# Two 64-byte gaps that shift the weights' split tiles off the 128-byte lines of SBUF

## The chip, the cores and the metric

The kernel runs on one core of a Trainium2 chip. The metric is the device time of one execution in microseconds (us), of which several are taken. Engines are named as in the profile: PE is TensorE's matmul, PEld its weight load, DVE is VectorE, ACT is ScalarE, POOL is GpSimd, SP issues the DMAs.

## What is computed

A decoder trunk of two layers on 256 positions with 1024 features, in float32. Layer 0 mixes tokens by dilated attention (16 heads, three groups of windows), layer 1 by an mLSTM block. After each mixer come an MLP with a squared ReLU and a gated input embedding.

```python
for i in range(2):
    if i == 0:
        x = x + dilated_attention(rms_norm(x, a_norm), a_w_qkv, ..., a_w_o)
    else:
        x = x + mlstm_mixer(rms_norm(x, b_norm), b_w_up, ..., b_w_down)
    x = x + jnp.square(jax.nn.relu(rms_norm(x, mlp_norm[i]) @ mlp_w1[i])) @ mlp_w2[i]
    gate = jax.nn.sigmoid(rms_norm(x, ple_norm[i]) @ ple_w_gate[i])
    x = x + gate * (p[i] @ ple_w_proj[i])
```

All the weights together are 138 units of 128 partitions by 2048 float32 (1 MB each). They are read from HBM once and used once, so the kernel is a long stream of weights past a small set of activations.

## The kernel before

**The stream of weights.** `dma(u)` (L161) brings unit u into one of three buffers `raw`. `split(u, c)` (L166) cuts a unit's 512-column piece into two float32r parts: ACT copies it to `hi` (L176), and DVE subtracts to get `lo` (L177). Twelve buffers each of `hi` and `lo` hold three units. One piece is a slot, and `open_slot` / `close_slot` (L209, L218) count slots: a split runs 7 slots ahead of its use during the attention projections and 11 afterwards. Work that isn't part of the stream (attention, gates, norms) is hung on slots with `at(slot, f)`.

**The products.** An activation h is kept as two parts as well (`hh` and `hl`, `hidh` and `hidl`, and so on), and each product is made of three matmuls: hi times hh, hi times hl, lo times hh. `stream` (L318) does this for most of the kernel. The weights' 128x128 piece is the stationary operand (512 bytes in a partition, loaded anew for every matmul), and the activation is the moving one (256 columns, 1024 bytes):

```python
mm(acc[:, q], wh, h, ...)   # L331
mm(acc[:, q], wh, l, ...)   # L332
mm(acc[:, q], wl, h, ...)   # L333
```

In the attention projections `qkv_block` (L483; matmuls on L499 to L501) it is the other way round: the activation is stationary, and the weights move, 512 columns at a time.

**The order.** A list of units written by hand sets it: `qkv` (36 units, slots with attention work between), `proj0`, `woA` and `woB` (the attention's output projection, moving operand `oT`), `w1_0` (moving `hh`), `w2_0` (moving `hid`), `gate0` (moving `hG`), `xm`, `z0` to `z3` (moving `hh`), `wd0` (moving `hB`), `proj1`, `wd1` (`hh`), `w1_1` (`hB`), `w2_1` (`hid`), `gate1` (`hh`). PE works through it in program order.

**Where the tiles lie.** Pools are laid out one after another from the bottom of SBUF: `base` (parameters, `hh`, `hl` and others), then `raw`, `hi`, `lo`, then the pool `sq`, and above it the pools of the stages in turn. A tile's start in a partition follows from the sizes before it. In the program as built, these are the starts of the rows counted modulo 128 bytes, for the operands of the matmuls:

| rows | used in | before | after the change |
|---|---|---|---|
| `hi`, `lo` (weights) | everywhere | 0 | 64 |
| `raw` | input of the split | 0 | 0 |
| `hh`, `hl` | qkv, w1_0, xm, z, wd1, gate1 | 0 | 0 |
| `hidh`, `hidl` | w2_0, w2_1 | 0 | 0 |
| `hBh`, `hBl` | wd0, w1_1 | 0 | 0 |
| `hWh`, `hWl` | four units of qkv | 0 | 0 |
| `oTh`, `oTl` | woA, woB | 64 | 64 |
| `hGh`, `hGl` | gate0 | 96 | 96 |
| `pT` (two parts) | proj0 / proj1 | 96 / 32 | 96 / 32 |

Every tile of these has rows that are whole multiples of 512 bytes, and so do the slices of them, so that a matmul's operand begins where its tile begins, modulo 128. Counted modulo 256 bytes, the distance from a row of weights to a row of activations (activation minus weights) was 0 for `hh`, `hid`, `hB` and `hW` and 192 for `oT`. After the change it is 192 for `hh`, 64 for `hid`, `hB` and `hW`, and 0 for `oT`.

Of the kernel before, what the change touches and what calls it, by code (L numbers as in the profile page):

```python
# [10 lines left out]
F32 = mybir.dt.float32  # L11
# [7 lines left out]
D, S, P = 1024, 256, 128  # L19
# [9 lines left out]
UC = 2048  # L29
HU = 512  # L30
# [102 lines left out]
def build(tc, a):  # L133
    nc = tc.nc
    ctx = ExitStack()
    with ctx:
        _build(ctx, tc, nc, a)


def _build(ctx, tc, nc, a):  # L140
    def pool(n, b=1, c=ctx, **k):
        if "space" not in k:
            k["reuse_waits"] = "tile"
        return c.enter_context(tc.tile_pool(name=n, bufs=b, **k))

    base = pool("base")
    rawp, hip, lop = pool("raw", 3), pool("hi", 3 * UC // HU), pool("lo", 3 * UC // HU)
    psa = pool("psa", 3, space=PSUM)
    pst = pool("pst", 2, space=PSUM)
    pss = pool("pss", 2, space=PSUM)  # L150
# [8 lines left out]
    raw, hi, lo = {}, {}, {}  # L159
# [188 lines left out]
    atp = pool("attn", c=actx)  # L348
# [170 lines left out]
    def scores(qt, i):  # L519

        pair, b = divmod(i, 2)
        tb = slice(b * P, (b + 1) * P)
        (qh, ql), (kh, kl) = QT[qt, 0], KTt[qt, 0]
        two = [(slice(r * HD, r * HD + HD), pss.tile([P, 512], F32, name="sc")[:, 0:SC]) for r in range(2)]
        for q, k, first, last in ((qh, kh, True, False), (qh, kl, False, False), (ql, kh, False, True)):
            for r, ps in two:
                mm(ps[:, 0:256], q[r, pair, tb], k[r, pair], start=first, stop=last)  # L527
        for n in range(2):
            for e in range(2):
                t4 = slice(b * P + 64 * e, b * P + 64 * e + 64)  # L530
                g = 1 + (n + e) % 2
                for r, ps in two:
                    mm(ps[64 * e:64 * e + 64, 256 + 64 * n:320 + 64 * n], QT[qt, g][0][r, pair, t4], KTt[qt, g][0][r, pair, t4],  # L533
                       start=True, stop=True)
        for r in range(2):
            j, ps = 2 * pair + r, two[r][1]
            sc = atp.tile([P, SC], F32, name="scs", bufs=2)
            m = atp.tile([P, 4], F32, name="m", bufs=8)
            slope = float(np.float32(2.0 ** (-8.0 * (4 * qt + j + 1) / H)))
            dve.tensor_tensor_reduce(sc, ps, nd[:, b], slope, -3e38, ALU.add, ALU.max, m[:, 0:1])  # L540
            dve.tensor_scalar(m[:, 1:2], m[:, 0:1], -1.0, None, op0=ALU.mult)
            act(sc, sc, AF.Exp, bias=m[:, 1:2], accum_out=m[:, 2:3])
            INST[qt, 2 * j + b] = (sc, m)
# [38 lines left out]
    def attend(qt, t0, step):  # L582
        for i in range(4):
            at(t0 + int((2 * i + 1) * step) + LV, values, qt, i)
        for i in range(4):
            for r in range(2):
                at(t0 + int((2 * i + r) * step) + LT, turn, qt, 4 * (i // 2) + 2 * r + i % 2)
        for i in range(4):
            at(t0 + int(2 * i * step), scores, qt, i)
        at(t0 + int(7 * step) + LV + 1, heads_done, qt)  # L590
# [484 lines left out]
```

## Time and profile before

| | |
|---|---|
| median of 3 runs | 923.03 us (921.54 to 923.29) |
| the profiled execution | 921.63 us, of which 919.9 us from the first to the last instruction |
| granted clock of TensorE, mean over the span | 0.997 of 2.4 GHz |
| PE busy / DVE busy / ACT busy | 98% / 72% / 62% of the span |
| read from HBM | 148 MB, 162 GB/s over the span |

A matmul's record in the profile is longer than the time until the next one starts, since matmuls are pipelined. What a matmul costs a stream that doesn't wait is therefore read as the step from one start to the next, not as the duration of one record.

### The profile page before, as it was taken

What the parts mean: (1) busy time and instruction counts of PE and PEld (TensorE: products, weight loads), DVE (VectorE), ACT (ScalarE), POOL (GpSimd) and SP (SyncE); (2) the same over time, 40 slices, a digit from 0 to 9 for tenths busy, and PEclk for the clock granted to TensorE, in tenths of its full rate; (3) what the DMA queues carried; (4) which work ended last, traced back from release to release, by engine and by line L of the source; (5) the groups of instructions that cost most, each with busy time, mean ns of one, the idle gap of its engine ahead of it and who ended that gap; (6) DMA issues with size and microseconds to landing.
All of it is one profiled execution on the core that took longest, in us unless ns stands there. A gap on an engine that the chain in (4) does not pass through costs nothing.

```text
span 919.9 us, 17609 instructions
## 1 busy us (share of the span) xinstructions
PE 904.3 (98%) x6924; PEld 844.3 (92%) x6924; DVE 659.7 (72%) x1409; ACT 569.5 (62%) x1055; POOL 41.5 (5%) x77
## 2 busy tenths in 40 slices
PE   8799999999999999999999999999999999999997
PEld 6687787877889999999999899999999999999997
DVE  6966877857866866665667987568898666656664
ACT  7567576575585766654446686668866666644442
POOL 0400000000000000000000542000000000000000
PEclk9999999999999999999999999999999999999999
DMA  8744443544443555555555433343265555555521
GB/s 302 281 142 160 156 144 133 178 136 145 154 161 105 178 185 183 184 183 184 183 184 183 157 129 104 127 138 98 87 220 204 184 183 184 184 183 182 184 94 46
DMA packets 23122, 150.23 MB, mean 163 GB/s; under 512 B 2560, under 2 KB 3200, under 8 KB 5632
## 3 DMA queue, kind: packets, MB, share of 16 engines
q1 hardware_dynamic: 23040, 149.12, 47.1%
q8 instruction: 54, 0.88, 0.4%
q14 instruction: 28, 0.23, 0.1%
HBM read 148.06 MB, written 1.05 MB: 162 GB/s over the span
## 4 chain that ended last, share of the span: by engine, by line
PE 92%; DVE 6%; ACT 1%; issue 1%; DMA 0%; SPq 0%; ACTq 0%
PE acc L331 21%; PE acc L332 21%; PE acc L333 21%; PE acc L499 6%; PE acc L501 6%; PE acc L500 6%; DVE lo L177 2%; PE tp L451 1%; PE tp L552 1%; PE sm L570 1%; PE sc L527 1%; PE tp L741 1%; PE tp L751 1%; PE sc L882 1%; PE sc L759 1%; PE sc L533 1%
## 5 line engine op out<-in xcount | busy, mean ns | idle before, releaser
L177 DVE TENSOR_TENSOR lo<-raw,hi 128x512 fp32r<-128x512 f32 x552 | 375.6, 691 | 176.7 <-ACT hi L176 175.3
L176 ACT ACTIVATE hi<-raw 128x512 fp32r<-128x512 f32 x552 | 339.2, 628 | 227.1 <-PE acc L332 204.4
L331 PE MATMUL acc<-hh,hi 128*128 128x256 f32 x640 | 184.0, 288 | 0.3 <-ACT hh L298 0.2
L332 PE MATMUL acc<-hl,hi 128*128 128x256 f32 x640 | 181.5, 284 | 0.1
L333 PE MATMUL acc<-hh,lo 128*128 128x256 f32 x640 | 181.4, 283 | 0.0
L331 PE MATMUL acc<-hidh,hi 128*128 128x256 f32 x512 | 144.9, 283 | 0.0
L332 PE MATMUL acc<-hidl,hi 128*128 128x256 f32 x512 | 144.9, 283 | 0.0
L333 PE MATMUL acc<-hidh,lo 128*128 128x256 f32 x512 | 144.9, 283 | 0.0
L331 PEld LDWEIGHTS acc<-hh,hi 128*128 128x128 f32 x640 | 122.4, 191 | 1.6 <-issue 0.7
L332 PEld LDWEIGHTS acc<-hl,hi 128*128 128x128 f32 x640 | 122.5, 191 | 0.7 <-DVE hl L299 0.5
L333 PEld LDWEIGHTS acc<-hh,lo 128*128 128x128 f32 x640 | 122.4, 191 | 0.0
L499 PE MATMUL acc<-hi,hh 128*128 128x512 f32 x264 | 109.6, 416 | 0.0
L500 PE MATMUL acc<-lo,hh 128*128 128x512 f32 x264 | 104.1, 394 | 0.8 <-DVE lo L177 0.8
L501 PE MATMUL acc<-hi,hl 128*128 128x512 f32 x264 | 104.2, 395 | 0.0
L331 PEld LDWEIGHTS acc<-hidh,hi 128*128 128x128 f32 x512 | 98.3, 192 | 0.0
L332 PEld LDWEIGHTS acc<-hidl,hi 128*128 128x128 f32 x512 | 98.3, 192 | 0.0
L333 PEld LDWEIGHTS acc<-hidh,lo 128*128 128x128 f32 x512 | 98.3, 192 | 0.0
L331 PE MATMUL acc<-hBh,hi 128*128 128x256 f32 x320 | 90.9, 284 | 0.0
L332 PE MATMUL acc<-hBl,hi 128*128 128x256 f32 x320 | 90.7, 283 | 0.0
L333 PE MATMUL acc<-hBh,lo 128*128 128x256 f32 x320 | 90.6, 283 | 0.0
L331 PEld LDWEIGHTS acc<-hBh,hi 128*128 128x128 f32 x320 | 61.4, 192 | 0.3 <-issue 0.3
L332 PEld LDWEIGHTS acc<-hBl,hi 128*128 128x128 f32 x320 | 61.4, 192 | 0.0
(258 smaller groups left out, 1384.3 us busy)
## 6 DMA issues: line engine op xcount, KB each, us to landing
raw<-w SPq DMA_DIRECT2D x136, 1024.0 KB, 4.9
raw<-w SPq DMA_DIRECT2D x8, 256.0 KB, 6.8
x<-x SPq DMA_DIRECT2D x4, 256.0 KB, 5.4
pj<-rep SPq DMA_DIRECT2D x1, 896.0 KB, 6.9
out<-u SPq DMA_DIRECT2D x3, 256.0 KB, 2.4
pT<-p SPq DMA_DIRECT2D x2, 256.0 KB, 4.0
nd<-nd SPq DMA_DIRECT2D x1, 384.0 KB, 6.2
out<-u SPq DMA_DIRECT2D x2, 128.0 KB, 1.9
```

The costliest lines, as they stand in the source:

```text
L176: act(hi[n][:, d], raw[u][:, s], AF.Copy)
L177: dve.tensor_tensor(lo[n][:, d], raw[u][:, s], hi[n][:, d], op=ALU.subtract)
L331: mm(acc[:, q], wh, h, start=first, stop=False, skip_group_check=n > 1)
L332: mm(acc[:, q], wh, l, start=False, stop=False, skip_group_check=n > 1)
L333: mm(acc[:, q], wl, h, start=False, stop=last, skip_group_check=n > 1)
L451: nc.tensor.transpose(ps[:, pair, b * P:(b + 1) * P], n[:, b, ty * 256 + pair * P:ty * 256 + (pair + 1) * P], ident)
L499: mm(accs[b], hh, wh, start=(k == 0), stop=False)
L500: mm(accs[b], hh, wl, start=False, stop=False)
L501: mm(accs[b], hl, wh, start=False, stop=(k == 7))
L527: mm(ps[:, 0:256], q[r, pair, tb], k[r, pair], start=first, stop=last)
L533: mm(ps[64 * e:64 * e + 64, 256 + 64 * n:320 + 64 * n], QT[qt, g][0][r, pair, t4], KTt[qt, g][0][r, pair, t4], start=True, stop=True)
L552: nc.tensor.transpose(psf[:, k * P:(k + 1) * P], pe[:, k * P:(k + 1) * P], ident)
```

## The change

A tile of 64 bytes in a partition (16 float32) that nobody uses is put ahead of the pools of `hi` and `lo`, and a second one behind them. All rows of `hi` and `lo` then begin 64 bytes higher, and all tiles above them 128 bytes higher. To make room for the 128 bytes, the small tile `m` of the attention's softmax (row maximum, its negative, sum, reciprocal), of which there were eight with one head each, becomes four with two heads each. No instruction is added, removed or moved on any engine, and each waits on the same semaphores as before.

```diff
     base = pool("base")
-    rawp, hip, lop = pool("raw", 3), pool("hi", 3 * UC // HU), pool("lo", 3 * UC // HU)
+    rawp = pool("raw", 3)
+
+    pool("gap0").tile([P, 16], F32, name="gap0")
+    hip, lop = pool("hi", 3 * UC // HU), pool("lo", 3 * UC // HU)
+    pool("gap1").tile([P, 16], F32, name="gap1")
     psa = pool("psa", 3, space=PSUM)
...
+        ms = atp.tile([P, 2, 4], F32, name="m", bufs=4)
         for r in range(2):
-            j, ps = 2 * pair + r, two[r][1]
+            j, ps, m = 2 * pair + r, two[r][1], ms[:, r]
             sc = atp.tile([P, SC], F32, name="scs", bufs=2)
-            m = atp.tile([P, 4], F32, name="m", bufs=8)
             slope = float(np.float32(2.0 ** (-8.0 * (4 * qt + j + 1) / H)))
```

## Rows read from the trace of the kernel before

**Rows 1.** The page's busy times of the engines.
```profile
PE 904.3 (98%) x6924; PEld 844.3 (92%) x6924; DVE 659.7 (72%) x1409; ACT 569.5 (62%) x1055; POOL 41.5 (5%) x77
```

**Rows 2.** The page's chain that ended last, shares of the span by engine.
```profile
PE 92%; DVE 6%; ACT 1%; issue 1%; DMA 0%; SPq 0%; ACTq 0%
```

**Rows 3.** Windows: start:end, length, busy of PE, PEld, DVE, ACT, POOL; clock, DMA, GB/s.
```profile
7.50:70.00 62.50, 56.43 (x253) 45.34 (x252) 49.46 (x116) 40.02 (x78) 12.66 (x21) 0.97 0.68 247
70.00:196.00 126.00, 126.00 (x826) 100.39 (x825) 94.50 (x250) 83.08 (x172) 0.00 (x0) 1.00 0.43 149
...
302.00:395.00 93.00, 93.00 (x775) 93.00 (x776) 67.82 (x111) 58.54 (x102) 0.00 (x0) 1.00 0.53 182
395.00:487.00 92.00, 92.00 (x769) 92.00 (x768) 55.09 (x90) 46.00 (x76) 0.00 (x0) 1.00 0.53 183
...
648.00:706.00 58.00, 58.00 (x477) 57.26 (x476) 52.42 (x116) 43.23 (x77) 0.00 (x0) 1.00 0.49 169
```

**Rows 4.** The chain in order of time: start, us, engine and work.
```profile
57.81 0.69 DVE nqk L443
...
503.75 1.44 DVE xn L697 x3
```

**Rows 5.** Line 331 in 395.5 to 487 (w2_0): duration min/median/max, first and last start.
```profile
L331 PEld LDWEIGHTS acc<-hidh,hi x255: 192/192/192, 395.4 to 486.8; 128*128 128x128 f32 x128
L331 PE MATMUL acc<-hidh,hi x255: 283/283/283, 395.5 to 486.9; 128*128 128x256 f32 x128
```

**Rows 6.** Line 331 in 294 to 301 (the end of the output projection, oT).
```profile
L331 PE MATMUL acc<-oTh,hi x21: 276/276/276, 293.9 to 300.7; 128*128 128x256 f32 x21
L331 PEld LDWEIGHTS acc<-oTh,hi x21: 187/188/188, 294.1 to 300.9; 128*128 128x128 f32 x21
```

**Rows 7.** Timeline of PE, a run of oT between attention work: start, us, work.
```profile
286.14 0.28 PE L332 MATMUL acc<-oTl,hi 128*128 128x256 f32 x1
...
287.32 0.28 PE L333 MATMUL acc<-oTh,lo 128*128 128x256 f32 x1
```

**Rows 8.** Line 331 over the whole output projection (270 to 301.7).
```profile
L331 PE MATMUL acc<-oTh,hi x64: 276/276/384, 270.3 to 301.4; 128*128 128x256 f32 x64
```

**Rows 9.** Line 331 in 489 to 499 (gate0, hG).
```profile
L331 PE MATMUL acc<-hGh,hi x27: 278/282/364, 488.7 to 499.0; 128*128 128x256 f32 x27
```

**Rows 10.** Timeline of PE in qkv, 16 steps on end.
```profile
243.48 0.39 PE L500 MATMUL acc<-lo,hh 128*128 128x512 f32 x1
...
247.15 0.39 PE L501 MATMUL acc<-hi,hl 128*128 128x512 f32 x1
```

**Rows 11.** The page's costliest groups: line engine op, count, busy, mean ns, idle before.
```profile
L177 DVE TENSOR_TENSOR lo<-raw,hi 128x512 fp32r<-128x512 f32 x552 | 375.6, 691 | 176.7 <-ACT hi L176 175.3
...
L331 PE MATMUL acc<-hh,hi 128*128 128x256 f32 x640 | 184.0, 288 | 0.3 <-ACT hh L298 0.2
...
L331 PE MATMUL acc<-hidh,hi 128*128 128x256 f32 x512 | 144.9, 283 | 0.0
...
L500 PE MATMUL acc<-lo,hh 128*128 128x512 f32 x264 | 104.1, 394 | 0.8 <-DVE lo L177 0.8
...
L331 PE MATMUL acc<-hBh,hi 128*128 128x256 f32 x320 | 90.9, 284 | 0.0
```

**Rows 12.** DVE's groups with shapes kept apart, two with 512 columns.
```profile
L264 DVE TENSOR_TENSOR sqa<-sqa,sqt 128x512 f32<-128x512 f32 x18 | 12.5, 695 | 0.3
...
L929 DVE TENSOR_TENSOR zt<-acc,rb 128x512 f32<-128x512 f32 x8 | 5.5, 682 | 0.5 <-PE acc L333 0.5
```

**Rows 13.** Timeline of PE at its longest wait: start, us, work, idle before.
```profile
44.89 0.45 PE L451 MATMUL tp<-ident,nqk 128*128 128x128 f32 x1 [5.02 <-DVE nqk L443]
```

## The prediction

> **What bounds the kernel now.** I read the page's busy times first: PE is busy for 98% of the span, with DVE at 72% and ACT at 62% [rows 1]. A busy PE alone proves little, so the chain that ended last comes next: 92% of it is PE, and DVE has 6% [rows 2]. The chain in order of time shows where that 6% lies: its DVE pieces stand before 58 us, and again for a short stretch around 500 to 516 us in `gate0` [rows 4]. Up to 45 us PE even stands still for 5.0 us behind DVE's `nqk` [rows 13], so nothing that PE wins before that point survives. From about 57 us on, PE is the bound. The windows by stage say how much room the others have there: in `w2_0` DVE works 55.1 of 92 us, in `w1_0` 67.8 of 93, in the attention projections 94.5 of 126. The tightest is the stretch from 648 to 706 with 52.4 of 58, that is 90% [rows 3]. So the time is a count of matmuls times the step from one to the next, and the question is what the change does to the step.
>
> **The step, and what the place of the rows has to do with it.** In `w2_0`, line 331 starts 255 times between 395.5 and 486.9 us; 254 rounds of three matmuls in 91.4 us are 762 steps of 120.0 ns. All its records have the same duration, 283 ns, and the weight loads 192 [rows 5]. At the end of the output projection the same line, with the same shapes and the same splits on DVE and ACT, starts 21 times from 293.9 to 300.7 us: 60 steps in 6.8 us, 113.3 ns each, with records of 276 and loads of 188 ns [rows 6]. The engines' clock was granted at 1.00 in both, which is 2.4 GHz. In the table of tiles the one thing that differs is that `oT` begins 64 bytes off the weights' lines, where `hid` begins on them. In qkv 512 columns take 16 steps in 3.67 us, 229.4 ns each [rows 10]. Against the 256 columns of `w2_0`, 256 columns more cost about 109 ns, so that a step of 120.0 holds some 11 to 13 ns over its columns, and `oT` loses about half of that.
>
> I take this as the mechanism: a weight load reads its row while the matmul before it reads its activation's row, and the two get in each other's way less when the rows stand 64 bytes apart modulo 128. The change puts `hh`, `hid` and `hB` where `oT` stood, and `oT` where they stood.
>
> The Trainium skill speaks against this. Its page "TensorE: Matmul & The Clock Gate", section "Part 2: What happens when you issue a matmul", says that loading the next tile's weights takes no read bandwidth of SBUF from the running matmul; its section "Back-to-back issue gap" would put an isolated matmul of 256 columns at 256/2.4 + 2.5 = 109 ns. By that rule both rows above would show 109, and the change would be worth nothing. The trace shows 120.0 and 113.3.
>
> **`oT` has a second rhythm.** A run between pieces of attention work goes from 286.14 to 287.32 us in 10 steps, which are 118 ns each [rows 7]. Which one a run falls into is set by how it starts, after a transpose or a small product, and it stays in it until the next interruption. Over the 192 matmuls of that stage [rows 8] about a quarter of the steps that follow each other closely are at 118, and the rest at 113.3. I take 0.75 x 113.3 + 0.25 x 118 = 114.5 ns for a stream 64 bytes apart. All fast would be 113.3, all slow 118. In the long undisturbed streams (`w1` and `w2`) one of them may hold for a whole stage, and no row tells which.
>
> **The change part by part.**
>
> *Streams whose activations start on the lines.* `hh` has 640 rounds, `hid` 512, `hB` 320 [rows 11]; with three matmuls each, 4416. Their mean records are 283 to 288 ns, as in `w2_0`, so they all run at 120.0. The gain is 4416 x (120.0 - 114.5) = 24.3 us; all fast 29.6, all slow 8.8.
>
> *The attention projections.* Line 500 has 264 matmuls on `hh` [rows 11], with 16 on `hW` and 8 into another buffer, so 288 on each of three lines, 864 in all; 700 of them start after 57 us. Here the weights move, and the activation is loaded, as far apart as `oT` was. No row has 512 columns at that distance: the gain lies between nothing and the 6.7 ns of the smaller matmul, as both have one weight load per matmul. I take the same 5.5, nearer to the row: 3.9 us (0 to 4.7). The 164 before that gain nothing, since DVE sets the end there [rows 13].
>
> *`oT`.* Its 64 rounds [rows 8] now stand on the weights' lines: 192 x (120.0 - 114.5) = 1.1 us lost (0.4 to 1.3).
>
> *`hG` and `pT`.* `hG` moves from 96 to 32 bytes apart. It now takes 26 rounds from 488.7 to 499.0 us [rows 9], 78 steps with two short waits, and its records lie between 276 and 283 like both others. 32 bytes could cost anything between 113.3 and 120.0: 0 to 1.3 us for 192 matmuls, and I take 0.4. The 96 matmuls of `pT` swap 32 for 96 in one layer and 96 for 32 in the other, and I put them at nothing (0.3 us either way).
>
> *The splits.* ACT and DVE now write, and DVE reads, rows at 64. DVE's subtract takes 691 ns with both operands at 0 [rows 11]; with one operand from PSUM a pass of 512 columns takes 682, with both from SBUF 695 [rows 12]. The place of the rows can hardly be worth more than that difference of 13 ns. PE's steps cover it: a slot of 12 matmuls falls from 1440 to 1374 ns, and `w2_0` would still have DVE at 55.1 of 88 us. Without that cover, 60 splits in the first 57 us would cost or give 0.8 us. I put it at nothing.
>
> *DVE's stretch.* From 500 to 516 us the chain goes over DVE [rows 4], and some 130 of the steps counted above gain nothing there: 0.5 us less.
>
> *The tile `m`* keeps its four pairs of buffers, and no wait is added. The DMA has to bring 1 MB in 5.5 instead of 5.76 us in `w1_0`, 191 GB/s for 182; it moved 247 GB/s between 7.5 and 70 us [rows 3]. Between 648 and 706 us PE would need 55.3 us and DVE 52.4, so PE still leads, barely.
>
> Sum: -24.3 - 3.9 + 1.1 - 0.4 + 0.5 = -27.0 us. The profiled execution's 921.63 us become 894.6. It stands 1.4 us under the median of the runs, so that 895 to 896 is the forecast; I say 895.
>
> **The rivals.**
>
> *The slow rhythm everywhere.* If the long streams settle at 118, the gain is 8.8 us there and 700 x 2 = 1.4 in qkv, less 0.4 for `oT`, and the time is about 913. For it: runs of ten steps held it to their end [rows 7]. Against it: the long run at the end of the stage was at 113.3 throughout [rows 6]. Chance 0.10.
>
> *Half of it.* If the distance counts modulo 256, then `oT` at 192 shows what `hh` will do, but nothing shows `hid` and `hB` at 64. If 64 is no better than 0, the 1920 matmuls of `hh` gain 10.6 us and qkv 3.9, `oT` loses 1.1, and the time is about 909. Against it: an exchange of the two rows should not matter. Chance 0.14.
>
> *No change.* If `oT` was fast for another reason, its own values or its place between other work, steps stay at 120 and the time at 923. Against it: DVE, ACT and DMA did the same work beside `oT` [rows 6] as elsewhere. It is also what the Trainium skill's page "SBUF — State Buffer", section "Specifications (TRN2)", suggests, where SBUF's lines are 16 bytes, of which 64 is a multiple; the 120.0 and 113.3 disagree with it as far as the tiles' places are their cause. Chance 0.05.
>
> *Slower.* A loaded row of 512 bytes covers four lines of 128 when it begins on one, and five when it doesn't. If the 13.3 ns over the columns are a price per line of the load, 3.3 each, the step becomes 123.3 and 4416 x 3.3 = 14.6 us are added, with 2.3 for the moving rows of qkv: 940. It decides as soon as `w1_0` shows steps over 120. Every load of `hi` or `lo` in the trace begins on a line, so no row of theirs excludes it; but `oT` moves 9 lines for 8 and was the faster one. Chance 0.06.
>
> **How the numbers follow.** The forecast has 0.65, and its own range goes from all fast in every stage (888) to half of the runs slow (about 901). Half of it and the slow rhythm reach to 909 and 913. The range from 888 to 912 takes in the first three cases but for their edges, some 0.85. A measurement of this kernel tells about 0.2%, 1.8 us, from no change. Forecast, slow rhythm and half make faster 0.89, the third rival same 0.05, the last slower 0.06.
>
> **What would show it.** In the profile after, `w2_0` should take about 87 us between the same units instead of 92, with steps of 113.3 and records of 276 and 188 ns, or 118 in whole stages. qkv should step at about 223 ns, `oT` at 120 with records of 283. PE stays at 97 or 98%, and DVE's split at 691. The prediction is wrong if `w1_0` and `w2_0` differ (then the distance counts modulo more than 128), if `oT` stays at 113.3 (then its place was not the cause), or if steps shrink and waits on `lo` or `hi` take what they gave.

## The result, and the profile after

The changed kernel takes 911.24 us (median of 4 runs, 909.07 to 913.14) against 922.43 us: a ratio of 0.9878, interval 0.9851 to 0.9905. It is 11 us faster, where 27 were forecast. The direction is right and the size is not. Line numbers after the change are four higher (331 is 335, 500 is 504).

The page's busy times of the changed kernel:

```profile
PE 894.8 (98%) x6924; PEld 833.9 (92%) x6924; DVE 659.2 (72%) x1409; ACT 568.5 (62%) x1055; POOL 39.4 (4%) x77
...
L181 DVE TENSOR_TENSOR lo<-raw,hi 128x512 fp32r<-128x512 f32 x552 | 375.3, 690 | 169.2 <-ACT hi L180 163.8
```

PE lost 9.5 us of busy time, and DVE and ACT kept theirs; the split of DVE takes 690 ns for 691 [rows 1, 11]. PE's longest wait on another engine is 4.9 us, where it was 5.0 [rows 13], and the others are no longer than before to within 0.3 us. So the whole of it is in the step from matmul to matmul, and the views of one line show it. First line 335 in w2_0, then in w1_0, then at the end of the output projection (oT):

```profile
L335 PE MATMUL acc<-hidh,hi x254: 278/279/280, 394.9 to 484.3; 128*128 128x256 f32 x127
L335 PEld LDWEIGHTS acc<-hidh,hi x253: 186/187/188, 395.2 to 484.2; 128*128 128x128 f32 x127
```
```profile
L335 PE MATMUL acc<-hh,hi x250: 280/281/364, 304.8 to 393.9; 128*128 128x256 f32 x125
```
```profile
L335 PE MATMUL acc<-oTh,hi x21: 283/284/284, 295.0 to 302.2; 128*128 128x256 f32 x21
```

In w2_0 253 rounds of three are 759 steps in 89.4 us: 117.8 ns, where it was 120.0 [rows 5] and 114.5 was forecast. oT has 60 steps in 7.2 us, 120 ns with records of 283, so it did take the others' old place [rows 6]. In qkv, the timeline of PE:

```profile
243.89 0.39 PE L504 MATMUL acc<-lo,hh 128*128 128x512 f32 x1
...
247.55 0.39 PE L505 MATMUL acc<-hi,hl 128*128 128x512 f32 x1
```

These are 16 steps in 3.66 us, 228.8 ns, against 229.4 [rows 10]. Over all the qkv steps after 57 us the mean is 230.0 ns for 229.3: the steps on hh went from 229.4 to 229.7, the few on hW from 227.8 to 233.3. The 3.9 us of that term did not come.

### The profile page after: what moved, and what is told of

Read it like the earlier page. It is cut to its first block, busy times and chain, and to the rows that moved or that the text cites. A ratio compares the mean times of both kernels' runs of the same rounds, so it can differ in the third digit from the quotient of the medians.

```text
span 910.5 us, 17609 instructions
## 1 busy us (share of the span) xinstructions
PE 894.8 (98%) x6924; PEld 833.9 (92%) x6924; DVE 659.2 (72%) x1409; ACT 568.5 (62%) x1055; POOL 39.4 (4%) x77
## 4 chain that ended last, share of the span: by engine, by line
PE 92%; DVE 6%; issue 1%; ACT 1%; DMA 0%; SPq 0%; ACTq 0%
PE acc L335 21%; PE acc L336 21%; PE acc L337 20%; PE acc L503 6%; PE acc L505 6%; PE acc L504 6%; DVE lo L181 2%; PE tp L455 1%; PE tp L556 1%; PE sm L574 1%; PE sc L531 1%; PE tp L745 1%; PE tp L755 1%; PE sc L886 1%; PE sc L763 1%
## 5 line engine op out<-in xcount | busy, mean ns | idle before, releaser
L337 PEld LDWEIGHTS acc<-hh,lo 128*128 128x128 f32 x640 | 120.3, 188 | 0.0
L336 PEld LDWEIGHTS acc<-hidl,hi 128*128 128x128 f32 x512 | 96.3, 188 | 0.0
L335 PEld LDWEIGHTS acc<-hidh,hi 128*128 128x128 f32 x512 | 96.2, 188 | 0.0
L337 PEld LDWEIGHTS acc<-hidh,lo 128*128 128x128 f32 x512 | 96.0, 188 | 0.0
L336 PE MATMUL acc<-hBl,hi 128*128 128x256 f32 x320 | 89.9, 281 | 0.0
L335 PE MATMUL acc<-hBh,hi 128*128 128x256 f32 x320 | 89.8, 281 | 0.0
```

The lines of the kernel that those rows point to most:

```text
L335: mm(acc[:, q], wh, h, start=first, stop=False, skip_group_check=n > 1)
L336: mm(acc[:, q], wh, l, start=False, stop=False, skip_group_check=n > 1)
L337: mm(acc[:, q], wl, h, start=False, stop=last, skip_group_check=n > 1)
```

## The experiments

"Distance" is from now on the one counted modulo 256 bytes, activation minus weights. For hG, which stays where it is in all kernels, it was 96 before and is 32 in the changed kernel. A "stretch" is a run of such matmuls that nothing interrupts. In the programs as built, the distances of the experiments are:

| kernel | hh | hid, hB | oT | hG |
|---|---|---|---|---|
| gap128 | 128 | 0 | 192 | 224 |
| off32 | 224 | 96 | 32 | 64 |
| off96 | 160 | 32 | 224 | 0 |
| up192 | 192 | 192 | 128 | 32 |
| all64 | 64 | 64 | 0 | 160 |

**The same kernel again.**

> The changed kernel itself once more, with a profile of its own. Theory A (two rhythms at a distance of 64 bytes, 113.3 and 117.8 ns a step; which of them a stretch of the stream falls into is decided where it starts, and it is kept until the next interruption): some long stage may show 113.3 this time where the first profile had 117.8; each stage of 768 matmuls that does so takes 3.4 us off, and the runs scatter between 905 and 914. Theory B (a long stream always settles at 117.8, and 113.3 lives only in short or often interrupted stretches): every long stage at 117.8 again, 909 to 913, and xm at 115 again.

Measured: 909.74 us (909.11 to 909.80), ratio 0.9861 (0.9844 to 0.9877). Line 335 in w1_0 this time, and the timeline of PE where w1_0 gives way to w2_0:

```profile
L335 PE MATMUL acc<-hh,hi x253: 276/276/367, 304.8 to 391.8; 128*128 128x256 f32 x127
```
```profile
391.64 0.28 PE L337 MATMUL acc<-hh,lo 128*128 128x256 f32 x1
...
392.32 0.28 PE L337 MATMUL acc<-hh,lo 128*128 128x256 f32 x1
392.44 0.28 PE L335 MATMUL acc<-hidh,hi 128*128 128x256 f32 x1
...
393.14 0.28 PE L335 MATMUL acc<-hidh,hi 128*128 128x256 f32 x1
```

The median record of w1_0 was 281 ns in the first profile and is 276 now. Up to the boundary 6 steps take 0.68 us (113.3), behind it 6 steps take 0.70 (117), with nothing in between but the change of the moving tile. So the same program ran w1_0 in one rhythm once and in the other the next time. Theory A holds for hh; but hid and hB stayed at 117.8 in both profiles, as theory B had it for every long stage.

Most places repeat, though. Of the 30 stretches of hh with 12 steps or more, 25 have the same rhythm in both profiles; in xm four stretches in a row have 117.9, 114.3, 113.9 and 114.3 ns, three times over, in the one profile as in the other. Only a few starts, that of w1_0 among them, went one way once and the other way the next time.

**Only the distance, in three sizes.** The gaps in floats (16 and 16 in the changed kernel):

```diff
 # gap128
-    pool("gap0").tile([P, 16], F32, name="gap0")
+    pool("gap0").tile([P, 32], F32, name="gap0")
-    pool("gap1").tile([P, 16], F32, name="gap1")
 # off32: gap0 [P, 8], gap1 [P, 24];  off96: gap0 [P, 24], gap1 [P, 8]
```

> The first gap is 128 bytes and the second is gone, so that hi and lo begin on the lines again while everything above them stands where the change puts it; the softmax tile of two heads stays. If the distance modulo 128 is all that matters: steps of 120.0 in all streams, 113 to 118 for oT, 922 to 923. If the other parts of the change (the tile m, the 128 bytes by which the upper pools move, the distance modulo 256, which is now 128 for hh and 0 for hid) have a share: w1_0 differs from w2_0, or the time lies outside 920 to 925.

> hi and lo begin at 32 of 128, the rest as in the changed kernel. The activations on the lines are then 96 bytes away modulo 128, as hG was before (119.9 ns a step), oT 32 and hG 64 away. If the distance decides as I think: steps of 120 in the long streams, 921 to 923, and hG at 113.3 or 117.8. If any place off the line would do: 117.8 as at 64, 911.

> hi and lo begin at 96 of 128. The activations on the lines are then 32 away, as pT of layer 1 was before (117.3 ns a step) and hG after the change (117.6); oT is 96 away and hG 0. If the distance decides: 117.5 in the long streams, 910 to 912, hG at 120. If a row of weights off the line by any amount is what helps, the same as the changed kernel and as 32; if 64 is the one good place, 922.

Measured: gap128 922.71 us, ratio 1.0006 (0.9996 to 1.0015); off32 922.67, 1.0003 (0.9993 to 1.0012); off96 913.63, 0.9904 (0.9890 to 0.9919). Line 334 or 335 in w2_0, in that order, and in w1_0 of gap128:

```profile
L334 PE MATMUL acc<-hidh,hi x251: 283/283/283, 398.9 to 488.9; 128*128 128x256 f32 x126
```
```profile
L335 PE MATMUL acc<-hidh,hi x251: 281/285/285, 397.9 to 487.9; 128*128 128x256 f32 x126
```
```profile
L335 PE MATMUL acc<-hidh,hi x252: 277/279/281, 398.1 to 485.9; 128*128 128x256 f32 x126
```
```profile
L334 PE MATMUL acc<-hh,hi x232: 279/281/364, 314.0 to 396.7; 128*128 128x256 f32 x116
```

Their steps are 90.0 us / 750 = 120.0, 90.0 / 750 = 120.0, and 87.8 / 753 = 116.6 ns. So the small tile, the upper pools' move and "off the line" as such leave `w2_0` at its old step; the distance doesn't. But gap128 shows that hh at 128 is not like hid at 0: records of 281 for 283, a mean step of 118.7. Its qkv went the other way, to 232.4 ns, and the two cancel in the time. The distance counts modulo 256, not 128. This is where the expectation of equal stages failed. off96 came out above its 910 to 912: hid has 116.6, but hh, at 160, has 117.8 in the mean, and qkv 233.7.

**All activations at 192, and the mirror image.**

```diff
 # up192: gap1 [P, 48];  all64: gap0 [P, 48]
-        v = atp.tile([P, 2, 8], F32, name="vqk", bufs=2)
-        dve.scalar_tensor_tensor(v, STAT["ss"], 1.0 / HD, ...)
+        v = STAT["ss"]
+        dve.scalar_tensor_tensor(v, v, 1.0 / HD, ...)
```

> The second gap is 192 bytes instead of 64, so that hid, hB and hW stand 192 bytes from the weights modulo 256, where hh stands already, instead of 64; oT goes from 0 to 128. (The 128 bytes come from the softmax of q and k: its variance is written over the sum of squares.) Theory A (the distance counts modulo 256: 192 has two rhythms, 113.3 and 117.8 ns, 64 has 117.8 alone): stretches of hid and hB at 113.3 appear for the first time; the 2496 matmuls take 4.4 ns less each where they do, and the time lies between 899 and 910, oT steps at 118.7. Theory B (modulo 128; hid and hB were slow by the chance of their starts): hid and hB as before, 117.8 in most stretches, 908 to 912.

> The mirror image: the first gap is 192 bytes and the second 64, so that hh, hid, hB and hW all stand 64 bytes from the weights modulo 256; the same room is taken as with 192. Theory A: no stretch of any stream at 113.3, all at 117.8; w1_0, xm, z and gate1 lose what they had, and the time is 913 to 916. Theory B: the same as with 192, with 113.3 in some stretches of hh, 908 to 912.

Measured: up192 904.59 us (903.71 to 905.05), ratio 0.9804 (0.9791 to 0.9818); all64 915.37, 0.9921 (0.9908 to 0.9935). Line 335 in w2_0 and in w2_1 of up192, then in w2_0 of all64:

```profile
L335 PE MATMUL acc<-hidh,hi x250: 276/276/276, 393.0 to 477.7; 128*128 128x256 f32 x125
```
```profile
L335 PE MATMUL acc<-hidh,hi x253: 281/281/281, 785.8 to 874.9; 128*128 128x256 f32 x127
```
```profile
L335 PE MATMUL acc<-hidh,hi x253: 280/280/280, 397.7 to 486.8; 128*128 128x256 f32 x127
```

In up192 layer 0 runs w2_0 in 747 steps of 113.4 ns, which no stage of hid had shown before, and layer 1 runs the same line in 756 steps of 117.9. Taken step by step, the first is one stretch of 1452 matmuls from the norm's last small product in w1_0 to the end of w2_0, all at 113.3; the second one of 1488 at 117.8. The four runs of up192 agree within 1.4 us, where one MLP in the other rhythm would be worth 6.5. all64 has 117.8 in its long streams. It did show 113.3 in 4 of its 36 stretches of hh (the longest 84 matmuls), so that "117.8 alone" for 64 was too strong: 113.3 is rare there, not absent.

**Can a start be chosen?** Two plain matmuls per MLP, behind the last small product of the norm. up192_kick has them on top of up192, kick64 in the changed kernel, up192_kick1 in layer 1 of up192 alone:

```diff
+        def kick():
+            ps = pst.tile([P, 2, S], F32, name="tp")
+            for i in range(2):
+                mm(ps[:, i], ones, prm[:, 0:S], start=True, stop=True)
+        at(clock[0] + SB + 2, kick)
         stream(B_W1, from_h(h1), mid)
```

> As with 192, and in each MLP's first half, two slots after the norm's factors are spread, PE gets two plain float32 matmuls of 256 columns (ones times parameters, a result that nobody reads), the form after which all twelve stretches of hh in the two profiles of the changed kernel ran at 113.3. They cost about 1 us each time. If the start of a stretch sets its rhythm: the rest of w1 and all of w2 at 113.3 in both layers, 2 x 1400 matmuls, 897 to 900, and less scatter from run to run. If the rhythm is not set there: as with 192 alone, 1 to 2 us more.

> The changed kernel with the same two matmuls put in, and no other gap. w1_0 (hh at 192) should run at 113.3 from there on, and w2_0, w1_1 and w2_1 (hid and hB at 64) at 117.8 in spite of them: 907 to 910. If hid and hB take 113.3 as well, it is the start alone and not the distance that kept them at 117.8: about 900.

> As with 192 everywhere, and the two plain float32 matmuls in the MLP of layer 1 alone, where they turned the rhythm from 117.8 to 113.3; in layer 0 they turned it the other way and are left out. If a start gives the same rhythm each time the same program runs: both MLPs at 113.3, 904.6 - 6.5 + 0.6 = about 899. If each build or each run draws anew: 898 to 910, with a scatter of several us.

Measured: up192_kick 907.77 us, ratio 0.9841 (0.9827 to 0.9854); kick64 914.70, 0.9916 (0.9903 to 0.9930); up192_kick1 903.99, 0.9801 (0.9771 to 0.9832). The timeline of PE around the kick in layer 0 of up192_kick, where the two matmuls show as four records:

```profile
316.64 0.28 PE L336 MATMUL acc<-hl,hi 128*128 128x256 f32 x1
316.75 0.28 PE L337 MATMUL acc<-hh,lo 128*128 128x256 f32 x1
316.87 1.03 PE L661 MATMUL tp<-prm,ones 128*128 128x256 f32 x4
...
317.97 0.28 PE L337 MATMUL acc<-hh,lo 128*128 128x256 f32 x1
...
318.56 0.28 PE L336 MATMUL acc<-hl,hi 128*128 128x256 f32 x1
```

Ahead of it the stream was at 113.3; after it 5 steps take 0.59 us, 118 each, and the next 1428 matmuls stayed there. In layer 1 the same kick turned 117.8 into 113.3 for 1464 matmuls. So an interruption can change the rhythm, but this one doesn't lead to a given one: the expectation of 113.3 behind it fell. kick64 agrees: w1_1 and w2_1 (64) stayed at 117.8 behind their kick, as expected, but w1_0 (192) went from 113.3 to 117.8, and the kernel is 3.5 to 5 us slower than in its two measurements without. In up192_kick1 the one kick again has 117.8 ahead of it and 113.3 behind. So each of the four profiled kicks at 192 had the other rhythm behind it than ahead. Whether a kick swaps the two or the rhythm is found afresh, four cases don't tell. The best runs are those of up192_kick1: 899.70, 899.72, 901.59, 906.39, 906.64 and 907.41 us. In its profile (901.59 us) both MLPs are at 113.3; line 335 in w2_0 and in w2_1:

```profile
L335 PE MATMUL acc<-hidh,hi x251: 276/276/276, 393.9 to 478.9; 128*128 128x256 f32 x126
```
```profile
L335 PE MATMUL acc<-hidh,hi x251: 276/276/276, 785.9 to 870.9; 128*128 128x256 f32 x126
```

The two groups of runs lie about 6.5 us apart, which is what one MLP's stretch of 1460 matmuls is worth (1460 x 4.45 ns = 6.5 us). That the slower three had one MLP at 117.8 is inferred from this; no profile was taken of them.

**Hi and lo apart.** A third gap stands between the two pools: 192 bytes in lo0, 64 in hi0 (which has none in front of hi and 192 behind lo), 32 in lo160. All three also have the `v` of up192. The edit for lo0, and the sizes in floats:

```diff
-    hip, lop = pool("hi", 3 * UC // HU), pool("lo", 3 * UC // HU)
+    hip = pool("hi", 3 * UC // HU)
+    pool("gapm").tile([P, 48], F32, name="gapm")
+    lop = pool("lo", 3 * UC // HU)
 # lo0: gap0 16, gapm 48, gap1 none;  hi0: none, 16, 48;  lo160: 16, 8, 40
```

> The gap of 192 bytes now stands between hi and lo: every activation is 192 from hi, but 0 from lo, modulo 256. Theory (a weight load meets the matmul that runs beside it): only the load of lo, one in three, meets its matmul on the same lines; in w2_0 the step of the line beside which it runs (332, whose record the load of lo follows by 2 to 4 ns) is longer, 120 or more, and the two others at 113 to 118, so that a round of three takes 347 to 356 ns, and the time lies between 908 and 917. If the place of the rows counts by itself and not for the pair, the three lines have equal steps.

> The reverse: activations 0 from hi and 192 from lo, modulo 256. By the theory line 332 keeps a step of 113 to 118 and lines 331 and 333, beside which hi is loaded, go to 120: a round of 353 to 358 ns, 914 to 920. If lo alone decides: 113.3 or 117.8 throughout.

> Activations 192 from hi and 160 from lo, a distance that showed 117.4 by itself. By the theory a round lies between 344 and 353 ns and the time between 904 and 912; a time under 903 would mean that unequal distances keep the stream from the slow rhythm.

Measured: lo0 917.74 us, ratio 0.9952 (0.9937 to 0.9967); hi0 915.40, 0.9925 (0.9912 to 0.9938); lo160 919.40, 0.9962 (0.9947 to 0.9976). Line 336, 336 and 337 in w2_0:

```profile
L336 PE MATMUL acc<-hidh,hi x255: 281/281/281, 397.0 to 486.7; 128*128 128x256 f32 x128
```
```profile
L336 PE MATMUL acc<-hidh,hi x255: 281/281/281, 395.8 to 485.6; 128*128 128x256 f32 x128
```
```profile
L337 PE MATMUL acc<-hidh,hi x253: 280/286/286, 397.9 to 487.8; 128*128 128x256 f32 x127
```

The steps are 117.7, 117.8 and 118.9 ns (89.7 and 89.8 us / 762, 89.9 / 756). In lo0 and hi0 the three lines have the same steps, 117 to 119, and none at 120: the theory that each load slows only the matmul beside it is refuted as it stood. In lo160 the lines do differ (120.4, 120.8 and 115.5 ns), but a round takes 357 ns, above the 344 to 353 expected, and the time is 7 us above its range. In lo0 the stretches from the end of wd0 through wd1 had 122.1 ns, more than any single distance had shown, while other stretches of the same tiles had 117.8: there, too, more than one rhythm belongs to one placing. The two distances act on a round together, and how is left open. Unequal ones were worse than 192 throughout, in every case tried.

## Why the prediction was wrong in its size

*The bound.* Right: PE at 98% before and after, and its step decides. The cover held as well: DVE's and ACT's busy times are unchanged, and up192 goes on to gain where the change stopped, so nothing but PE limits the long streams.

*That the place of the rows sets the step.* Right as a relation between two rows, shown by moving only the weights under hG, which itself never moved: it ran at 120 at a distance of 0 (off96) and 117.8 at 64 (off32). In gap128 weights and hid both stand 128 bytes from their old places modulo 256, and the step is 120.0 as before. Three different tiles at 224 (hh in off32, oT in off96, hG in gap128) gave 118.2 to 118.3. oT fell back to 120 as foreseen, for about 1 us. The step that "a weight load reads its row while the matmul before it reads its activation's row" is not confirmed in detail; lo0 and hi0 speak against its simplest form.

*The term that failed: "4416 x (120.0 - 114.5) = 24.3 us".* Its 114.5 rested on three steps in four being fast, as in the one stage of oT. The 4416 matmuls gained 2.6 ns each instead of 5.5: 11.5 us by stages (w1_0, w2_0, w1_1 and w2_1 1.7 each, xm and z 3.3, the rest 1.4). Two reasons, each with its runs. First, "64 bytes apart modulo 128" was taken for one thing, on the ground that an exchange of the two rows should not matter, and it is two: oT's distance was 192 modulo 256, and hid and hB, 2496 of the 4416 matmuls, were put at 64, where 113.3 hardly occurs (hid and hB had it in no stretch of the changed kernel's two profiles). The rival *half of it* named this case, but priced 64 at no gain at all; it is worth 2.2 ns. up192 shows it: with those at 192 too, 6.6 us more than the change (5.2 against its second measurement). Second, a long stage has one rhythm, not a mean over many. In the profile w1_0 had 117.8, in the next one 113.3 (3.4 us for 765 steps). That a start sets the rhythm, as the prediction says, fits the stretches that repeat; for w1_0 what stands ahead of it doesn't settle it. The rival *slow rhythm everywhere* had the right size for the four MLP stages; xm, interrupted every few microseconds, had a mean of 115.2, near the 114.5 of the forecast.

That 911.24 still lies inside the stated range is owed to the rivals at 909 and 913, not to the sum. The sign that was to show a distance counted modulo more than 128, a difference between w1_0 and w2_0, was missing in the first profile, where w1_0 happened to run at hid's 117.8, and came in the second.

*qkv.* "I take the same 5.5" was wrong. With 512 columns moving, 192 gives no gain (hh has 229.7 ns for 229.4); other distances cost 3 to 4 ns more: 232.4 in gap128, 233.1 in off32, 233.7 in off96. Nor was oT's place the same as hh's here: in qkv the activation is the loaded row, so that, counted as moving minus loaded, oT stood at 192 and hh now stands at 64. The other order gives no gain either: in all64, where moving minus loaded is 192, hh has 233.3. The lower bound of that term, nothing, was the right value.

*The others.* hG fell from 119.9 to 117.6 ns, the 0.4 us that were taken, though no row had given that figure. The splits cost nothing (690 ns for 691), and the tile m nothing that shows (gap128: 1.0006). The rival *slower* is excluded: the long streams got faster with the weights off the line, and off32, off the line as well, has the old 120.0 in w2_0. *No change* is excluded by the steps: 113.3 to 120.0 ns for one shape at a granted clock of 1.00, by the distance between the loaded and the moving row and, at 192, by the start. The Trainium skill says ("TensorE: Matmul & The Clock Gate", "Part 2: What happens when you issue a matmul") that loading the next tile's weights takes no SBUF read bandwidth from the running matmul. By that rule alone these steps would be equal, and they aren't; that it is read bandwidth that is lost is not shown.

## What to carry to other kernels

Where PE streams matmuls that each load new weights, compare the step from start to start between stages of one shape; if it differs, look at where the operands' rows start relative to each other, modulo 256 bytes, before looking for waits. A gap tile of a few bytes is then a cheap trial, but try several distances and read the step in every stage, since one stage's good distance isn't another's. When a trace shows two values side by side, a long uninterrupted stage will have one of them, not their mean: price it as the one or the other, and profile more than once.

## What the runs showed of the hardware that was not expected

Mean step of 256-column float32r matmuls with a load for each in w1_0 and w2_0, by distance modulo 256: 0: 120.0 (before); 32: 116.7 (off96); 64: 117.8 (changed kernel); 96: 120.0 (off32); 128: 118.7 (gap128); 160: 117.3 (off96); 192: 113.3 (up192) or 117.8 (w1_0 of the changed kernel); 224: 118.3 ns (off32). Most records go along (276 ns at 113.3, 283 at 120.0), but the profile models where a matmul ends, so the step is the measure.

Other distances than 192 have more than one value as well: 32 has 117.7 and 116.7 in two stretches of gate0 in the changed kernel, 128 has 118.7 in w1_0 of gap128 and 120.0 in a later stretch of 82 steps, 160 has 118.7 in wd1 of off96. The list is of single long stages, not of all that a distance can show.

At 192 there are two rhythms, 113.3 and 117.8, and no stretch was seen to change from one to the other between two interruptions, not in 1488 matmuls. A change of the moving tile's distance in mid-stream, without a gap, changes the step at once.

The steps do not follow what DVE and ACT do meanwhile: in w2_0 every round of three takes 360 ns before and 340 in up192, with DVE busy for 60% of that stage before [rows 3].

Left open: what in a start picks the rhythm, why 192 and 64 differ, and whether it is reads of a round that get in each other's way, and which.
